# A 31-tap depthwise convolution as three half-length ones on VectorE, inside a two-block kernel

## The chip, the cores and the metric

One NeuronCore of a Trainium2 chip runs the whole program. The metric is the device time of one execution in microseconds; the runs shown are three of the same kernel, and a profiled execution is a fourth. The names of engines are those of the profile: PE is TensorE, DVE is VectorE, ACT is ScalarE, POOL is GpSimd, SP is the queue of SyncE.

## The reference

Two blocks follow each other on x (1024 tokens, width 1024). The first is a mixer, a cross-attention and a squared-ReLU MLP; nothing in it is touched. The second starts with one projection that is cut into nine pieces for four mixers, whose outputs are concatenated, projected and followed by a gated MLP:

```
z_pool, s_b, s_c, s_h, c_a, c_g, zq, zk, zv = split(rms_norm(x) @ w_in)
u      = c_a * sigmoid(c_g)                      # 256 channels
u      = causal_dwconv(u, conf_dw_w) + conf_dw_b # 31 taps, every channel its own
y_conf = silu(layer_norm(u))
y_attn = differential attention: softmax(q1 k1) - lam * softmax(q2 k2), times v   # 4 heads
x      = x + concat(y_pool, y_sconv, y_conf, y_attn) @ w_out
```

The change touches two places: the 31-tap convolution behind `u`, and in the attention the one number per query by which the second softmax is scaled before it is added to the first, `-lam * sum1 / sum2`.

## The kernel before, in words

All activations are kept channels by tokens: a tile of 128 x 1024 f32 holds 128 channels (partitions) and all 1024 tokens. A matrix product splits each f32 operand into a rounded part and a remainder and issues three matmuls of 512 columns per 128 rows of depth; the weight's remainder `wl` is computed by POOL (from `wr` and `wh`), activations' remainders by DVE. DVE reads each product out of PSUM (`gm`).

The program is written as Python generators ("tasks") that a small planner, `drive`, interleaves: it takes the task of the lowest priority number whose awaited tiles are ready by the planner's clock for TensorE, and issues its instructions up to the next `yield`. The clock prices a DVE instruction at 0.065 us plus 1.04 ns a column, a POOL one at 0.05 us plus 2.2 ns a column; it does not let one engine slow another. What it issues is then the order on each engine, up to a short window within which the scheduler may exchange instructions (24 for DVE, 8 for ACT and POOL; PE keeps its order). Each engine takes its instructions strictly in that order.

In `second`, the projection is the task of priority 10, so it fills PE when nothing else is ready. ORDER2 lists its pieces: attention pair 0, convolution 0, sconv 1, convolution 1, sconv 0, attention pair 1, pool 1, pool 0. Heads run as tasks of priority 2, their value part in `attn_value`, and the two convolutions (128 channels each) as tasks of priority 3 in `conf_in`.

`conf_in` (line 2233) gates `ca` with the sigmoid of `cg`, then builds the sum over 31 taps in two accumulators. On DVE, taps 0 to 20: ACT writes tap 0 with the bias into `cy`, and 20 instructions add a shifted and scaled copy of the input, each over about 1010 columns, two of them between two yields (line 2247). On POOL, taps 21 to 30: ACT writes tap 21 into a second accumulator (also named `cy` in the trace), and for each of the other nine ACT makes a scaled copy `ctap` (line 2253) and POOL adds it (line 2254). One DVE addition joins the two accumulators (line 2257). When both convolutions are done, `conf_out` normalises them, and their results go to DRAM and come back for the output projection.

`attn_value` (line 2149) is the tail of one block of 128 queries: a reciprocal of the two row sums (`ars`), the column factor (`ars<-asm,nlam,ars`, one column, line 2157), one DVE instruction that adds the second softmax to the first with that factor (`ap<-ap,ars`, up to 1024 columns, line 2159), then PE transposes the result (`apt`), ACT copies it (`aT`), and PE multiplies by v (`apo`). At the end of a head pair DVE normalises `ao` and PE transposes it (`yaT`).

Of the kernel before, what the change touches and what calls it, by code (L numbers as in the profile page):

```python
# [11 lines left out]
AF = mybir.ActivationFunctionType  # L12
ALU = mybir.AluOpType
# [23 lines left out]
G_CONV, G_ONORM, G_POOL, G_SC, G_CW, G_CB, G_CG, G_CBB, G_QG, G_KG = 56, 104, 105, 107, 113, 175, 177, 179, 181, 182  # L37
# [7 lines left out]


PRI = 200

CONF_POOL = 10

QD = 2

# [150 lines left out]
class Kern:  # L203
# [1945 lines left out]
    def attn_value(self, ao, vT, qt, P, sm, done):  # L2149
        nc = self.nc  # L2150
        n = (qt + 1) * 128

        rs = self.small("ars", 4)
        yield [sm]
        nc.vector.reciprocal(rs[:, 0:2], sm)
        yield [rs]
        nc.vector.scalar_tensor_tensor(rs[:, 2:3], sm[:, 0:1], self.nlam, rs[:, 1:2], ALU.mult, ALU.mult)
        yield [rs]
        nc.vector.scalar_tensor_tensor(P[0], P[1], rs[:, 2:3], P[0], ALU.mult, ALU.add)
        P = P[0]  # L2160
        aT = None
        for c0 in range(0, n, 512):
            c1 = min(n, c0 + 512)
            yield [P, self.free_s()]
            if aT is None:
                aT = self.u("aT")
            pt = self.s("apt")
            for kb in range(0, (c1 - c0) // 128):
                o = c0 + kb * 128
                nc.tensor.transpose(pt[:, kb * 128:kb * 128 + 128], P[:, o:o + 128], self.ident)  # L2170
            nc.scalar.activation(aT[:, c0:c1], pt[:, :c1 - c0], AF.Copy)
        del P
        yield [aT, self.free_s()]
        po = self.s("apo")
        for kb in range(qt + 1):
            nc.tensor.matmul(po[:, 0:64], aT[:, kb * 128:kb * 128 + 128], vT[:, kb * 64:kb * 64 + 64], start=(kb == 0), stop=(kb == qt))
        nc.scalar.activation(ao[:, qt], po[:, 0:64], AF.Copy, scale=rs[:, 0:1])
        done.set(ao)
# [52 lines left out]
        self.y_set(j, y)  # L2231

    def conf_in(self, j, a, g_):
        nc, gv = self.nc, self.gv
        nc.scalar.activation(g_, g_, AF.Sigmoid)
        nc.vector.tensor_tensor(a, a, g_, ALU.mult)
        y, y2 = self.u("cy"), self.u("cy2")
        w = G_CW + 31 * j
        nc.scalar.activation(y, a, AF.Identity, scale=gv[:, w + 30:w + 31], bias=gv[:, G_CB + j:G_CB + j + 1])

        first = 31 - CONF_POOL
        tap = lambda d: gv[:, w + 30 - d:w + 31 - d]
        nc.gpsimd.memset(y2[:, 0:first], 0.0)
        nc.scalar.activation(y2[:, first:], a[:, :1024 - first], AF.Copy, scale=tap(first))
        far = list(range(first + 1, 31))
        for d in range(1, first):
            nc.vector.scalar_tensor_tensor(y[:, d:], a[:, :1024 - d], tap(d), y[:, d:], ALU.mult, ALU.add)
            if d % 2 == 0:
                yield [y]
                if far:  # L2250
                    f = far.pop(0)
                    p = self.u("ctap")
                    nc.scalar.activation(p[:, f:], a[:, :1024 - f], AF.Copy, scale=tap(f))
                    nc.gpsimd.tensor_tensor(y2[:, f:], y2[:, f:], p[:, f:], ALU.add)
        assert not far
        yield [y2]
        nc.vector.tensor_tensor(y, y, y2, ALU.add)
        self.cu[j] = y
        self.ev_cu[j].set(y)

# [160 lines left out]
```

## Time and profile before

| what | value |
|---|---|
| three runs | 2655.64, 2653.11, 2649.26 us, median 2653.11 us |
| the profiled execution | 2642.57 us, of which the span of the trace is 2640.9 us |
| mean granted TensorE clock | 0.981 |
| busy: PE, DVE, ACT, POOL | 2509.0, 1578.5, 871.9, 891.5 us |

Times in the trace are microseconds from the start of the span. Busy PE is the time in which at least one matmul is under way. The second block's projection, attention and convolutions lie at about 1500 to 1900 us. The names `cy` and `pl` occur in other stages too, so a row on them is read with its stretch.

### The profile page before, as it was taken

The page shows a single profiled execution, that of the slowest core. Times are in us where ns is not written, and L with a number is a line of the kernel's source. Part 1 is how long each engine was busy: PE and PEld are TensorE (multiplying, and loading weights), DVE is VectorE, ACT ScalarE, POOL GpSimd, SP SyncE. Part 2 cuts the span into 40 slices and gives each one's busy share as a digit, 9 for nine tenths or more (in the row PEclk, how much of TensorE's full clock was granted, in tenths as well). Part 3 has the DMA queues.
Part 4 walks back from the last instruction along what each step waited for, and adds up shares of the span by engine and source line. Part 5 has one row for each costly group of instructions (what it writes and reads, how often), then busy time and mean ns, then how long its engine had stood idle before and what let it go on. Part 6 is the DMA issues. An engine that isn't in the chain of part 4 may idle for free. (4 is left out here: it accounts for less than half of the span.)

```text
span 2640.9 us, 30371 instructions
## 1 busy us (share of the span) xinstructions
PE 2509.0 (95%) x11880; PEld 2056.6 (78%) x11880; DVE 1578.5 (60%) x2249; ACT 871.9 (33%) x1234; POOL 891.5 (34%) x376
## 2 busy tenths in 40 slices
PE   8999999999999999999999889888969999999999
PEld 6878877888877888778888667667847888887887
DVE  7972767554456666553435767976586666564433
ACT  5422343233343333321213434434453222222210
POOL 1121121211244454322222442521175556653221
PEclk9999999999999999999999999899979999999999
DMA  3322146421232333642211331033221222226212
GB/s 128 88 83 74 64 159 214 170 88 47 70 124 82 118 104 120 231 137 97 97 56 48 118 91 56 32 130 100 78 85 64 88 88 80 80 97 251 91 49 88
DMA packets 99135, 268.26 MB, mean 102 GB/s; under 512 B 19976, under 2 KB 34480, under 8 KB 98992
## 3 DMA queue, kind: packets, MB, share of 16 engines
q1 hardware_dynamic: 78400, 192.40, 21.3%
q10 hardware_dynamic: 20592, 73.93, 8.4%
q8 instruction: 93, 1.52, 0.2%
q14 instruction: 50, 0.41, 0.1%
HBM read 196.55 MB, written 69.74 MB: 101 GB/s over the span
## 5 line engine op out<-in xcount | busy, mean ns | idle before, releaser
L184 POOL TENSOR_TENSOR wl<-wr,wh 128x1024 fp32r<-128x1024 f32 (+1 forms) x137 | 340.9, 2489 | 1299.0 <-ACT wh L184 1235.2
L184 DVE TENSOR_TENSOR x<-gm,x 128x512 f32<-128x512 f32 x304 | 209.0, 688 | 355.9 <-PE gm L184 355.6
L184 ACT ACTIVATE wh<-wr 128x1024 fp32r<-128x1024 f32 (+2 forms) x147 | 153.0, 1042 | 610.0 <-PE gm L184 575.7
L184 PE MATMUL gm<-fhh,wh 128*128 128x512 f32 x864 | 337.7, 391 | 3.4 <-ACT fhh L184 2.5
L184 PE MATMUL gm<-fhl,wh 128*128 128x512 f32 x864 | 337.1, 390 | 1.5 <-DVE fhl L184 1.4
L184 PE MATMUL gm<-fhh,wl 128*128 128x512 f32 x864 | 336.6, 390 | 0.0
L184 PE MATMUL gm<-hh,wh 128*128 128x512 f32 x800 | 325.0, 407 | 11.8 <-ACT hh L184 7.7
L184 PE MATMUL gm<-hl,wh 128*128 128x512 f32 x800 | 319.8, 400 | 0.5 <-DVE hl L184 0.5
L184 PE MATMUL gm<-hh,wl 128*128 128x512 f32 x800 | 319.0, 399 | 0.0
L184 PEld LDWEIGHTS gm<-fhh,wh 128*128 128x128 f32 x864 | 162.2, 188 | 41.5 <-ACT fhh L184 3.3
L184 PEld LDWEIGHTS gm<-fhl,wh 128*128 128x128 f32 x864 | 162.3, 188 | 36.0 <-DVE fhl L184 3.1
L184 PEld LDWEIGHTS gm<-fhh,wl 128*128 128x128 f32 x864 | 162.3, 188 | 33.9
L184 PEld LDWEIGHTS gm<-hh,wh 128*128 128x128 f32 x800 | 153.7, 192 | 44.4 <-ACT hh L184 8.6
L184 PEld LDWEIGHTS gm<-hh,wl 128*128 128x128 f32 x800 | 153.7, 192 | 32.5 <-issue 0.5
L184 PEld LDWEIGHTS gm<-hl,wh 128*128 128x128 f32 x800 | 153.8, 192 | 31.1 <-DVE hl L184 1.9
L184 POOL TENSOR_TENSOR wl<-pr,wh 128x1024 fp32r<-128x1024 f32 x38 | 91.6, 2410 | 118.1 <-ACT wh L184 118.1
L184 POOL TENSOR_TENSOR wl<-sa,wh 128x1024 fp32r<-128x1024 f32 x38 | 92.9, 2446 | 106.5 <-ACT wh L184 106.5
L184 PE MATMUL q<-tl,wh 128*128 128x512 f32 x304 | 120.6, 397 | 6.6 <-POOL tl L184 6.6
L184 PE MATMUL q<-th,wl 128*128 128x512 f32 x304 | 120.7, 397 | 4.6 <-POOL wl L184 4.6
L184 PE MATMUL q<-th,wh 128*128 128x512 f32 x304 | 119.3, 394 | 3.5 <-ACT th L184 2.6
L184 POOL TENSOR_TENSOR pl<-sb,ph 128x1024 fp32r<-128x1024 f32 x38 | 92.8, 2443 | 86.2 <-ACT ph L184 86.1
L184 DVE TENSOR_TENSOR fhl<-fhr,fhh 128x1024 fp32r<-128x1024 f32 x54 | 91.3, 1696 | 29.8 <-ACT fhh L184 29.8
(445 smaller groups left out, 5328.0 us busy)
## 6 DMA issues: line engine op xcount, KB each, us to landing
fhr<-hd SPq DMA_DIRECT2D x54, 512.0 KB, 5.1
wr<-in_w_in_dram ACTq DMA_DIRECT2D x39, 512.0 KB, 3.5
xd<-x SPq DMA_DIRECT2D x32, 512.0 KB, 2.6
x<-xd SPq DMA_DIRECT2D x32, 512.0 KB, 4.6
pr<-in_ffn_w_dram SPq DMA_DIRECT2D x32, 512.0 KB, 3.6
wr<-in_ffn_w_dram ACTq DMA_DIRECT2D x32, 512.0 KB, 3.5
hd<-ft SPq DMA_DIRECT2D x27, 512.0 KB, 5.0
hd<-pc SPq DMA_DIRECT2D x27, 512.0 KB, 5.8
```

The source lines that it names most:

```text
L184: ins = f(*args, **kw)
```

## The change

The convolution is written over even tokens, odd tokens and their sums. With a0 and a1 the even and odd tokens (512 columns each), h0 the 16 even taps and h1 the 15 odd ones, three convolutions over 512 columns are made: p0 = h0 * a0, p1 = h1 * a1, p2 = (h0 + h1) * (a0 + a1). Even outputs are p0 plus p1 delayed by one, odd outputs are p2 - p0 - p1. ACT writes the first tap of each, DVE all others: 15, 14 and 15 instructions, of 497 to 511 columns, three (at the last step two) between two yields. POOL has no part in it any more, and the copies `ctap` are gone. New on DVE are the sums of neighbouring taps (16 columns), the sum a0 + a1, and four instructions that put the result together; the gating multiplication now reads its two inputs at every second column and writes halves, and two of the last four write every second column.

In `attn_value` the column factor is one `tensor_scalar` with two column operands in place of a `scalar_tensor_tensor`.

```diff
-CONF_POOL = 10
...
-        nc.vector.scalar_tensor_tensor(rs[:, 2:3], sm[:, 0:1], self.nlam, rs[:, 1:2], ALU.mult, ALU.mult)
+        nc.vector.tensor_scalar(rs[:, 2:3], sm[:, 0:1], self.nlam, rs[:, 1:2], ALU.mult, ALU.mult)
...
     def conf_in(self, j, a, g_):
         nc, gv = self.nc, self.gv
+        apart = lambda x: x.rearrange("p (n h) -> p h n", h=2)
+        w = G_CW + 31 * j
+        hs = self.small("hs", 16)
+        pairs = gv[:, w + 1:w + 31].rearrange("p (m o) -> p m o", o=2)
+        nc.vector.tensor_tensor(hs[:, 1:16], pairs[:, :, 0], pairs[:, :, 1], ALU.add)
+        nc.vector.tensor_copy(hs[:, 0:1], gv[:, w:w + 1])
         nc.scalar.activation(g_, g_, AF.Sigmoid)
-        nc.vector.tensor_tensor(a, a, g_, ALU.mult)
-        y, y2 = self.u("cy"), self.u("cy2")
-        w = G_CW + 31 * j
-        nc.scalar.activation(y, a, AF.Identity, scale=gv[:, w + 30:w + 31], bias=gv[:, G_CB + j:G_CB + j + 1])
-        first = 31 - CONF_POOL
+        ab = self.u("cab")
+        nc.vector.tensor_tensor(ab.rearrange("p (h n) -> p h n", h=2), apart(a), apart(g_), ALU.mult)
+        yield [ab]
+        sc, y2 = self.u("csc"), self.u("cy2")
+        a0, a1, both = ab[:, :512], ab[:, 512:], sc[:, :512]
+        nc.vector.tensor_tensor(both, a0, a1, ALU.add)
         tap = lambda d: gv[:, w + 30 - d:w + 31 - d]
-        nc.gpsimd.memset(y2[:, 0:first], 0.0)
-        nc.scalar.activation(y2[:, first:], a[:, :1024 - first], AF.Copy, scale=tap(first))
-        far = list(range(first + 1, 31))
-        for d in range(1, first):
-            nc.vector.scalar_tensor_tensor(y[:, d:], a[:, :1024 - d], tap(d), y[:, d:], ALU.mult, ALU.add)
-            if d % 2 == 0:
-                yield [y]
-                if far:
-                    f = far.pop(0)
-                    p = self.u("ctap")
-                    nc.scalar.activation(p[:, f:], a[:, :1024 - f], AF.Copy, scale=tap(f))
-                    nc.gpsimd.tensor_tensor(y2[:, f:], y2[:, f:], p[:, f:], ALU.add)
-        assert not far
-        yield [y2]
-        nc.vector.tensor_tensor(y, y, y2, ALU.add)
+        parts = [(y2[:, :512], a0, lambda k: tap(2 * k), 16), (y2[:, 512:], a1, lambda k: tap(2 * k + 1), 15), (sc[:, 512:], both, lambda k: hs[:, 15 - k:16 - k], 16)]
+        for y, x, t, n in parts:
+            nc.scalar.activation(y, x, AF.Copy, scale=t(0))
+        for k in range(1, 16):
+            for y, x, t, n in parts:
+                if k < n:
+                    nc.vector.scalar_tensor_tensor(y[:, k:], x[:, :512 - k], t(k), y[:, k:], ALU.mult, ALU.add)
+            yield [y2, sc]
+        y = self.u("cy")
+        ya = apart(y)
+        bias = gv[:, G_CB + j:G_CB + j + 1]
+        p0, p1, p2 = (part[0] for part in parts)
+        nc.vector.scalar_tensor_tensor(ya[:, 0, 1:], p0[:, 1:], bias, p1[:, :511], ALU.add, ALU.add)
+        nc.vector.tensor_scalar(ya[:, 0, 0:1], p0[:, 0:1], bias, None, ALU.add)
+        nc.vector.tensor_tensor(p0, p0, p1, ALU.add)
+        nc.vector.scalar_tensor_tensor(ya[:, 1], p2, bias, p0, ALU.add, ALU.subtract)
```

## Rows read from the trace of the kernel before

**Rows 1.** The page, part 1: busy us, share of the span, instructions.

```profile
PE 2509.0 (95%) x11880; PEld 2056.6 (78%) x11880; DVE 1578.5 (60%) x2249; ACT 871.9 (33%) x1234; POOL 891.5 (34%) x376
```

**Rows 2.** Windows: stretch, length, busy PE, PEld, DVE, ACT, POOL, granted clock, DMA, GB/s.

```profile
1541.00:1607.00 66.00, 52.97 (x245) 43.53 (x243) 61.94 (x54) 28.85 (x51) 36.50 (x15) 0.92 0.20 56
1607.00:1651.00 44.00, 41.76 (x253) 35.97 (x252) 29.03 (x51) 22.98 (x52) 4.83 (x3) 1.00 0.14 49
1651.00:1723.00 72.00, 55.08 (x256) 44.95 (x255) 67.34 (x63) 27.07 (x40) 38.20 (x14) 0.91 0.09 29
1820.00:1880.00 60.00, 60.00 (x374) 52.76 (x374) 35.96 (x70) 32.99 (x79) 6.00 (x3) 1.00 0.28 93
```

**Rows 3.** Waits of PE, 1541 to 1723: us in total, times, longest.

```profile
PE apt L184 <- DVE ap L184: 14.8, 5, 4.7
PE apt L184 <- DVE ars L184: 6.1, 2, 4.3
```

**Rows 4.** DVE's groups, 1541 to 1723: out<-in xcount | busy us, mean ns | idle before.

```profile
L184 DVE SCALAR_TENSOR_TENSOR cy<-ca,gv,cy 128x1023 f32<-128x1023 f32 (+19 forms) x40 | 71.5, 1789 | 1.5 <-ACT cy L184 1.2
L184 DVE SCALAR_TENSOR_TENSOR ap<-ap,ars,ap 128x640 f32<-128x640 f32 (+3 forms) x8 | 17.1, 2133 | 0.1
L184 DVE SCALAR_TENSOR_TENSOR ars<-asm,nlam,ars 128x1 f32<-128x1 f32 x16 | 14.1, 888 | 0.2
L184 DVE SCALAR_TENSOR_TENSOR ap<-ap,ars 128x128 f32<-128x128 f32 (+3 forms) x8 | 8.4, 1055 | 0.1
L184 DVE TENSOR_SCALAR ass<-ass 128x8 f32<-128x8 f32 x2 | 2.0, 1006 | 0.0
```

**Rows 5.** Timeline of DVE: start us, us, instruction, count.

```profile
1564.11 2.58 DVE L184 SCALAR_TENSOR_TENSOR cy<-ca,gv,cy 128x1015 f32<-128x1015 f32 x2
...
1566.72 3.32 DVE L184 SCALAR_TENSOR_TENSOR cy<-ca,gv,cy 128x1013 f32<-128x1013 f32 x1
...
1571.11 0.67 DVE L184 TENSOR_TENSOR sh<-gm,sc 128x512 f32<-128x512 f32 x1
1571.70 1.08 DVE L184 SCALAR_TENSOR_TENSOR ars<-asm,nlam,ars 128x1 f32<-128x1 f32 x1
1572.70 1.26 DVE L184 SCALAR_TENSOR_TENSOR cy<-ca,gv,cy 128x1012 f32<-128x1012 f32 x1
1573.89 2.65 DVE L184 SCALAR_TENSOR_TENSOR ap<-ap,ars 128x384 f32<-128x384 f32 x1
...
1714.96 1.23 DVE L184 TENSOR_TENSOR cy<-cy,cy 128x1024 f32<-128x1024 f32 x1 [2.22 <-POOL cy L184]
```

**Rows 6.** Timeline of POOL over the same stretch.

```profile
1566.63 2.35 POOL L184 TENSOR_TENSOR cy<-cy,ctap 128x1000 f32<-128x1000 f32 x1 [2.48 <-ACT ctap L184]
1570.36 2.40 POOL L184 TENSOR_TENSOR wl<-wr,wh 128x1024 fp32r<-128x1024 f32 x1 [1.39 <-ACT wh L184]
1573.82 2.30 POOL L184 TENSOR_TENSOR cy<-cy,ctap 128x999 f32<-128x999 f32 x1 [1.06 <-ACT ctap L184]
```

**Rows 7.** POOL's groups, 1541 to 1723.

```profile
L184 POOL TENSOR_TENSOR cy<-cy,ctap 128x1002 f32<-128x1002 f32 (+8 forms) x18 | 49.4, 2747 | 44.2 <-ACT ctap L184 43.9
L184 POOL TENSOR_TENSOR wl<-wr,wh 128x1024 fp32r<-128x1024 f32 x9 | 22.7, 2517 | 63.4 <-ACT wh L184 63.4
L184 POOL TENSOR_TENSOR sh<-sh,r1b 128x1024 f32<-128x1024 f32 x2 | 6.0, 3019 | 0.0
```

**Rows 8.** DVE's groups by form, 1800 to 1890, where POOL does little.

```profile
L184 DVE SCALAR_TENSOR_TENSOR ars<-asm,nlam,ars 128x1 f32<-128x1 f32 x16 | 3.5, 216 | 0.3
...
L184 DVE SCALAR_TENSOR_TENSOR ap<-ap,ars 128x512 f32<-128x512 f32 x2 | 1.5, 752 | 0.0
```

**Rows 9.** Windows: one wait of PE, and the stretch right behind it.

```profile
1582.50:1586.00 3.50, 0.21 (x2) 0.07 (x1) 3.50 (x3) 0.00 (x0) 2.85 (x1) 1.00 0.99 249
1586.70:1590.10 3.40, 3.40 (x9) 2.64 (x9) 3.40 (x5) 1.17 (x3) 0.00 (x0) 0.50 0.28 70
```

**Rows 10.** The only DVE TENSOR_SCALAR of one full column, by its tile.

```profile
L184 DVE TENSOR_SCALAR nlam<-nlam x1: 145/145/145, 1450.4 to 1450.4; 128x1 f32<-128x1 f32 x1
```

## The prediction, made before the changed kernel ran

> **What bounds the kernel now.** I read the page's first part, then windows over the second block, then PE's waits there, then DVE and POOL side by side in the timeline. PE is busy 95% of the span [rows 1], so time can only come from stretches in which it isn't. The two convolutions are such stretches: PE is busy 52.97 of 66 us and 55.08 of 72 us, 30.0 us idle together, while DVE is busy 94% [rows 2]. Between the two the same attention and projection run with 2.2 us idle in 44, and later with none in 60, DVE being at 66% and 60%: the idle time belongs to a saturated DVE, not to the attention's own chain. PE waits there 20.9 us for two DVE results, `ap` and `ars` [rows 3]; the rest falls on several others. A second loss stands beside it. The granted clock is 0.92 and 0.91 in the two stretches and 1.00 outside [rows 2], which is 66 x 0.08 + 72 x 0.09 = 11.8 us of full-speed work. Right behind a wait of 3.5 us in which PE did 0.21 us of work, a stretch of 3.4 us ran at 0.50, the lower level of 1.2 GHz [rows 9]; the clock fell when PE had stood still.
>
> **Why DVE is saturated.** A tap of 1012 columns takes 1.26 us when it runs freely, and 3.32 us when POOL's addition of a tap, begun 0.09 us before it, is under way: POOL ends at 1568.98, the tap at 1570.04, one free duration later [rows 5, 6]. So does `ap` at 1573.89, behind POOL's 1573.82 [rows 5, 6]. Even the one-column `ars` averages 0.888 us here against 0.216 us where POOL does little [rows 4, 8]. A DVE instruction that reads two SBUF tiles stands until POOL's is over. Reckoned over both stretches, with free durations of 0.752 us at 512 columns and 1.26 at 1012 (1.02 ns a column) [rows 5, 8]: taps 71.5 - 40 x 1.27 = 20.7; the long `ap` (832 columns in the mean, 1.08 us) 17.1 - 8.6 = 8.5; the short ones (320, 0.56 us) 8.4 - 4.4 = 4.0; `ars` 14.1 - 3.5 = 10.6; `ass` about 1.7 [rows 4, 8]. Sum 45.5 us in which DVE stood, of its 129.3 busy. POOL's work there is 49.4 us of taps, 22.7 of `wl` and 6.0 of `sh` [rows 7]; taps are 63%, which gives them 28.8 of the 45.5 us.
>
> **The change part by part.**
>
> *POOL's taps go.* DVE gains 28.8 us over the two convolutions, and ACT loses one copy per tap. DVE's wait of 2.22 us for POOL's last tap, with a head pair's tail queued behind it, goes too [rows 5].
>
> *DVE's taps.* Before, 40 in all; DVE begins the next instruction 0.08 us before the end of one whose result it doesn't need (1571.11 to 1571.70 for 0.67 us), and 0.04 us behind the end of one whose result it does (two taps in 2.58 us) [rows 5]. A tap so occupies 1.19 to 1.31 us; most are followed by another instruction, I take 1.22: 24.5 us per convolution. After, 44 of 504 columns in the mean, 0.742 us each. Three accumulators alternate, so no tap needs the one ahead: 0.66 us, 29.0 per convolution. Should two halves of a tile count as one, it is 0.78, 34.3 per convolution. I take the first, nearest to the 0.59 us of a 512-column instruction in [rows 5]. Difference +4.5, at most +9.8, at least +2.8 per convolution.
>
> *The other additions on DVE, per convolution.* The sum a0 + a1 0.59 us; the two small ones on taps 0.2; at the end two of 0.67, one of 0.59 and one of a column 0.1, against 1.15 for the old join. Together +1.7. The gating multiplication keeps its count of elements. That it and two of the last four step over every second column is in no row; bounds: nothing, or twice their time per element, +2.2. I take nothing, since the row nearest to it, a dense 512-column one, shows no cost but columns. The Trainium skill (SBUF - State Buffer, section "Door 1: The DMA port swizzle") says that reads which meet a 16-byte line at least twice run at full rate; f32 at a step of two does so, and by that page the term is nothing too. No run here shows it yet.
>
> Sum on DVE: 2 x (4.5 + 1.7) = +12.4 against -28.8, net -16 us of 129 (bounds -1 to -20).
>
> *The column factor.* `tensor_scalar` of one column took 145 ns [rows 10], `scalar_tensor_tensor` 216 [rows 8]: 16 x 0.07 = 1.1 us in these stretches if it holds, at most 10.6 if the new form never stands behind POOL. But then `ap`, the next on its chain, stands behind the same POOL instruction instead, and a TENSOR_SCALAR, `ass`, was also held (1.006 us in the mean) [rows 4]. I count nothing.
>
> *ACT and POOL.* ACT's six first taps become half as wide; both engines have room (ACT 28.85 of 66 us, POOL 36.50) [rows 2]. Nothing.
>
> **From DVE to the end.** PE's order is fixed, and it has other work at 100% once its waits are gone (1820 to 1880 in [rows 2]). So what it doesn't wait, the span loses. Of PE's 30.0 us the taps' 63% give 19. The added 12.4 us are in the planner's prices for the most part (0.59 against 0.66 us a tap) and displace attention by little; POOL's blocks are in no price, and that is what made PE late. The clock's 11.8 us goes with the waits in the same share, 7 us. Total 26 us. The new DVE work may bring back some waits: at -1 us net on DVE the gain would be only what smoother order brings, some 5; and with all waits and the whole clock back it would be 42. What is late next: `wl` and `sh`, whose 28.7 us of POOL stay, and then the attention's loads.
>
> The profiled execution took 2642.6 us, the median of the runs is 2653.1, 10.5 higher. By the profile the sum gives 2616.6, on the scale of the runs 2627.
>
> **The rivals.** A measurement of this kernel can tell about 0.2%, 5.3 us, from no change.
>
> *The rest of POOL blocks more.* Nearly every instruction that DVE now has reads two SBUF tiles and is short, so that whenever `wl` or `sh` runs, one stands at the head of the queue. Before, a microsecond of POOL held DVE for 45.5 / 78.1 = 0.58 us. At 1.0, the 28.7 us left hold it for 28.7 instead of 16.7, DVE's relief falls from 16 to 4 us, and the gain in that proportion from 26 to 6.5: 2647. For it: taps make up half of DVE's instructions' time in [rows 4]. Against: DVE also reads PSUM in the projection and the maxima, which did not stand (0.67 at 1571.11 beside a POOL run [rows 5, 6]). The Trainium skill (SBUF - State Buffer, section "Who interferes with whom") has the pair of ports as a lock for a whole instruction, the loser blocked entirely; by that rule the price of a `wl` can't shrink with the width of the tap it meets, and the trace agrees: beside the `wl` of 1570.36 the one-column `ars` took 1.08 us and ended with it [rows 5, 6].
>
> *DVE takes more than it gives back (slower).* Forty-four instructions at their start-to-start cost, alone on DVE, behind which the heads' `ap` queue. Place: the same two stretches. It decides from (16 / 88) + 0.66 = 0.84 us a tap on; 0.78 doesn't reach it, but a step of two charged at each read or a wait on the first ACT tap could. At 1.0 us DVE has 14 us more than before, PE's waits grow by the 30 / 45.5 that a blocked microsecond cost so far, +9 us, and the clock with it: 2665. For: DVE is at 94% already. Against: 0.59 us for 512 columns.
>
> *All comes back.* No wait left, full clock: 2653 - 42 = 2611. For: the stretches without taps. Against: `wl` still holds DVE.
>
> **How the numbers follow.** The forecast (15 to 36 us of gain, own range 2617 to 2638) 0.57; all comes back 0.13; the rest of POOL blocks more, or the planner's new order brings other waits, 0.20, of which two thirds lie within 0.2%; slower 0.10. So faster 0.77, same 0.13, slower 0.10. The range runs from 2610 (nearly all) to 2650 (the weak case): the slower case and the edge of the others stay out.
>
> **What would show it.** In the profile after: no `ctap`, and 88 taps near 0.74 us with starts 0.66 apart; POOL's busy time down by 49 us or more; the sum of `ap` and `ars` near free durations, except beside `wl`; PE's waits for `ap` and `ars` under a third; the granted clock above 0.97 in both stretches. I am wrong if the taps stand 0.8 us apart, if PE's idle time in the convolutions stays near 30 us, or if it reappears between the convolutions and the output projection.

## The result and the profile after

The changed kernel takes 2618.07 us in the median of four runs (2615.66 to 2618.96), the kernel before 2654.29 us in the four beside it (2649.26 to 2655.64). The ratio is 0.9872, 95% interval 0.9855 to 0.9889: 36 us less, where 26 were forecast and 2627 us named, inside the range of 2610 to 2650. The profiled execution after is one of the four, 2618.96 us with a span of 2616.7.

First the windows of the kernel after: the two convolutions, now at 1545 to 1625 and 1625 to 1705, and the stretch behind them (columns as in [rows 2]).

```profile
1545.00:1625.00 80.00, 75.66 (x408) 63.39 (x406) 71.99 (x109) 32.57 (x72) 15.36 (x7) 1.00 0.22 66
1625.00:1705.00 80.00, 73.50 (x391) 60.72 (x389) 77.56 (x119) 30.52 (x59) 16.48 (x7) 1.00 0.15 51
1705.00:1723.00 18.00, 12.06 (x39) 8.49 (x40) 16.21 (x35) 5.86 (x7) 4.67 (x2) 0.72 0.02 10
```

PE's idle time in the convolutions is 4.34 + 6.50 = 10.8 us, against 30.0 in [rows 2], and the granted clock is 1.00 in both instead of 0.92 and 0.91. DVE is no less busy than before, 90% and 97% against 94%: what fell is not its busy share but PE's waits for what comes out of it. These windows don't hold the same work as those of [rows 2]: the matmuls that stood in the 44 us between the two convolutions now run inside them. The third window shows what is left: PE is idle 5.94 us behind the convolutions, and there the clock falls to 0.72. PE's waits from 1545 to 1723 say the same, against 20.9 us for `ap` and `ars` in [rows 3]; `ars` is gone from the list.

```profile
PE apt L182 <- DVE ap L182: 7.1, 3, 3.0
PE gm L182 <- DVE zqk L182: 2.9, 2, 2.3
PE cm L182 <- DVE zv L182: 2.4, 1, 2.4
```

The groups of DVE from 1535 to 1725, which answer to [rows 4]. The taps of p0 and p1 are named `cy`, those of p2 `csc`; the row `cab<-ca,cg` is the gating, which reads at every second column, and `cy<-csc,gv,cy` the odd outputs, written at every second column.

```profile
L182 DVE SCALAR_TENSOR_TENSOR cy<-cab,gv,cy 128x511 f32<-128x511 f32 (+14 forms) x58 | 47.3, 841 | 0.0
L182 DVE SCALAR_TENSOR_TENSOR csc<-csc,hs 128x511 f32<-128x511 f32 (+14 forms) x30 | 26.1, 869 | 0.0
...
L182 DVE SCALAR_TENSOR_TENSOR ap<-ap,ars,ap 128x640 f32<-128x640 f32 (+3 forms) x8 | 8.6, 1077 | 0.0
...
L182 DVE SCALAR_TENSOR_TENSOR ap<-ap,ars 128x128 f32<-128x128 f32 (+3 forms) x8 | 6.2, 772 | 0.1
...
L182 DVE TENSOR_SCALAR ars<-asm,nlam,ars 128x1 f32<-128x1 f32 x16 | 4.3, 266 | 0.1
...
L182 DVE TENSOR_TENSOR cab<-ca,cg 128x1024 f32<-128x1024 f32 x2 | 2.4, 1216 | 2.6 <-ACT cg L182 2.6
...
L182 DVE SCALAR_TENSOR_TENSOR cy<-csc,gv,cy 128x512 f32<-128x512 f32 x2 | 1.5, 748 | 0.0
```

The eight long `ap` have come from 17.1 us down to 8.6, their free time; `ars` from 14.1 to 4.3. The timelines of DVE and of POOL over one stretch show the taps in step and what still holds them: taps begin 0.66 us apart (1560.40, 1561.06, and two in 1.32), until POOL's `wl` and `sh` stand in the way of two of them (1566.28 and 1568.55).

```profile
1560.40 0.74 DVE L182 SCALAR_TENSOR_TENSOR csc<-csc,hs 128x511 f32<-128x511 f32 x1
1561.06 1.41 DVE L182 SCALAR_TENSOR_TENSOR cy<-cab,gv,cy 128x510 f32<-128x510 f32 x2
1562.38 0.74 DVE L182 SCALAR_TENSOR_TENSOR csc<-csc,hs 128x510 f32<-128x510 f32 x1
...
1566.28 2.35 DVE L182 SCALAR_TENSOR_TENSOR cy<-cab,gv,cy 128x508 f32<-128x508 f32 x1
1568.55 2.88 DVE L182 SCALAR_TENSOR_TENSOR csc<-csc,hs 128x508 f32<-128x508 f32 x1
```

```profile
1565.70 2.39 POOL L182 TENSOR_TENSOR wl<-wr,wh 128x1024 fp32r<-128x1024 f32 x1 [9.22 <-ACT wh L182]
1568.04 2.85 POOL L182 TENSOR_TENSOR sh<-sh,r1b 128x1024 f32<-128x1024 f32 x1
```

The gain lies in one stretch. From the first transpose of the attention's norms (`zb`) to the first matmul of the output projection (`gm<-yh,wh`) the kernel before takes 295.3 us and the kernel after 264.7, which is 30.6 less (the two profiles differ by 24.2 us in all; experiment 4 takes up the rest). These are the windows of that stretch, first before, then after. PE's records of matmuls are as many in both, 1223, so here like is compared with like: its idle time falls from 41.5 to 20.1 us, and its busy time, which a lower clock lengthens, from 253.8 to 244.6.

```profile
1498.20:1793.50 295.30, 253.76 (x1223) 206.92 (x1224) 219.77 (x275) 118.35 (x188) 113.07 (x45) 0.94 0.28 88
```

```profile
1501.50:1766.20 264.70, 244.56 (x1223) 200.51 (x1224) 208.27 (x336) 97.53 (x170) 61.96 (x25) 0.96 0.31 98
```

### The profile page after: what moved, and what is told of

The parts are those of the page before. It is cut to its first block, busy times and chain, and to the rows that moved or that the text cites. A ratio compares the mean times of both kernels' runs of the same rounds, so it can differ in the third digit from the quotient of the medians.

```text
span 2616.7 us, 30367 instructions
## 1 busy us (share of the span) xinstructions
PE 2500.9 (96%) x11880; PEld 2053.4 (78%) x11880; DVE 1564.9 (60%) x2309; ACT 853.3 (33%) x1218; POOL 840.0 (32%) x356
```

## The experiments

Theory: POOL's additions of taps, which read SBUF, made DVE's instructions on two SBUF tiles stand, `ap` and `ars` among them, for which PE waited. Rivals: fewer copies on ACT; a finer order through half-length taps; less work on DVE; the column factor. Times are medians; "before" is the kernel before, run beside each experiment. "Stretch" is the one just named.

**1. POOL writes, but reads nothing.**

```diff
-                    nc.gpsimd.tensor_tensor(y2[:, f:], y2[:, f:], p[:, f:], ALU.add)
+                    nc.gpsimd.memset(self.u("cz")[:, f:], 0.0)
```

> The kernel before, with one thing changed: where POOL added a tap (it read two SBUF tiles), it now fills a scratch tile with zeros, so it only writes. ACT's copies, DVE's 20 full-width taps per convolution and the planner's prices stay. Taps 22 to 30 are left out of the result. Theory (POOL's reads hold DVE): DVE's taps come down from 1.79 us to about 1.35 in the mean, since only wl and sh still hold them, DVE gets some 29 us back and the time falls by 25 to 40 us against before, 2614 to 2629. Rival (the gain comes from fewer ACT copies, from halving the taps or from a smoother order): no more than 5 us, 2648 or above, taps still near 1.8 us.

2619.41 us, ratio 0.9868 (0.9844 to 0.9892), as much as the whole change, with DVE's full-width taps and ACT's copies in place. The groups of POOL and of DVE, 1541 to 1723:

```profile
L184 POOL MEMSET cz<- 128x1002 f32 (+8 forms) x18 | 16.2, 930 | 0.0
...
L184 DVE SCALAR_TENSOR_TENSOR cy<-ca,gv,cy 128x1023 f32<-128x1023 f32 (+19 forms) x40 | 53.6, 1340 | 0.5
```

The taps' mean is 1.34 us instead of 1.79. So none of the rivals is needed for the size of the gain. But POOL is also less busy here, 16.2 us of fills against 49.4 of additions, so that reading and being busy aren't told apart yet.

**2. All 30 taps on DVE at full width.**

```diff
-        first = 31 - CONF_POOL
...
-        for d in range(1, first):
+        for d in range(1, 31):
...
-                if far:
...
-        yield [y2]
-        nc.vector.tensor_tensor(y, y, y2, ALU.add)
```

> The kernel before with all 30 further taps on DVE at full width, two between two yields, no POOL and no copies: the same result as before, without the half-length form. Theory: POOL's 29 us of holding are gone, but 20 more taps of 1.2 us, 24 us, come to DVE; the net is about 5 us less DVE, and as the planner prices the added taps but not the holding, the time falls by 5 to 20 us against before, 2634 to 2649. Then the half-length form is worth the rest, 16 to 31 us. Rival (taking POOL out is all that counts, DVE's own sum isn't): as the changed kernel, 2618 within 5.

2631.20 us, ratio 0.9908 (0.9884 to 0.9932): faster than before by 22 us, 3 us better than the theory's 5 to 20 against the 2653.75 us beside it, and 13 us slower than with half-length taps, where 16 to 31 were expected. Adding 20 taps to DVE still pays, since they only take its time, while POOL's additions hold its queue. DVE's taps, 1545 to 1720:

```profile
L184 DVE SCALAR_TENSOR_TENSOR cy<-ca,gv,cy 128x1023 f32<-128x1023 f32 (+29 forms) x60 | 86.2, 1437 | 0.6
```

**3. The old companions back, to no use, in the changed kernel.**

```diff
+            if k < 10:
+                p = self.u("ctap")
+                nc.scalar.activation(p[:, 21 + k:], ab[:, :1003 - k], AF.Copy, scale=tap(21 + k))
+                nc.gpsimd.tensor_tensor(z[:, 21 + k:], z[:, 21 + k:], p[:, 21 + k:], ALU.add)
```

> The changed kernel with the old companions put back, to no use: for each convolution ACT makes nine scaled copies of about 1000 columns, and POOL adds them into a scratch tile that nobody reads. Theory: DVE, which now has 12 us more of its own work than before, is held by POOL again for about 29 us, PE's waits for ap come back, and the time rises by 25 to 45 us, to 2643 to 2663, near or above before. Rival (halved taps and their finer order made the gain): within 8 us of the changed kernel, below 2626.

2653.06 us, ratio to before 0.9998 (0.9985 to 1.0012). The whole gain is gone, though the halved taps and their finer order are all there. `ars` is never held in this run, and `ap` only little; what the additions hold are above all the taps, which take 94.3 us in place of 73.4, and PE waits for `ap` all the same. POOL's additions, DVE's taps and PE's waits, 1545 to 1740:

```profile
L182 POOL TENSOR_TENSOR cz<-cz,ctap 128x1002 f32<-128x1002 f32 (+8 forms) x18 | 46.5, 2582 | 56.2 <-ACT ctap L182 47.8 <-DMA stk<-qkd 8.0
```

```profile
L182 DVE SCALAR_TENSOR_TENSOR cy<-cab,gv,cy 128x511 f32<-128x511 f32 (+14 forms) x58 | 53.8, 948 | 0.0
L182 DVE SCALAR_TENSOR_TENSOR csc<-csc,hs 128x511 f32<-128x511 f32 (+14 forms) x30 | 40.5, 1350 | 0.0
...
L182 DVE SCALAR_TENSOR_TENSOR ap<-ap,ars,ap 128x640 f32<-128x640 f32 (+3 forms) x8 | 12.2, 1520 | 0.0
L182 DVE SCALAR_TENSOR_TENSOR ap<-ap,ars 128x128 f32<-128x128 f32 (+3 forms) x8 | 6.3, 782 | 0.1
...
L182 DVE TENSOR_SCALAR ars<-asm,nlam,ars 128x1 f32<-128x1 f32 x16 | 4.2, 262 | 0.0
```

```profile
PE apt L182 <- DVE ap L182: 20.8, 5, 8.5
PE gm L182 <- DVE ca L182: 6.0, 1, 6.0
PE gm L182 <- DVE zqk L182: 4.0, 1, 4.0
```

**4. The kernel before, profiled again.** Nothing is edited.

> The kernel before, unchanged, for a second profile: the one shown took 2642.6 us, the runs 2649 to 2656. If the ten microseconds lie in the convolutions, then how POOL's and DVE's instructions meet varies from run to run: PE's idle time there is 35 to 40 us instead of 30. If they lie elsewhere (loads, the second MLP), the idle time in the convolutions is 30 within 2, and the gain of the change on the scale of the profiles is the 24 us that the two profiles show.

2652.92 us, the usual time of that kernel. Its windows over the stretches of [rows 2], and over the stretch from `zb` to the output projection:

```profile
1541.00:1607.00 66.00, 52.31 (x242) 43.27 (x241) 58.28 (x53) 29.77 (x50) 37.30 (x15) 0.90 0.20 56
1607.00:1651.00 44.00, 42.11 (x251) 36.44 (x250) 28.15 (x50) 22.81 (x54) 5.27 (x3) 0.96 0.11 37
1651.00:1723.00 72.00, 57.52 (x273) 46.83 (x271) 68.46 (x52) 28.07 (x41) 39.20 (x16) 0.93 0.12 37
```

```profile
1502.90:1800.30 297.40, 254.68 (x1224) 208.84 (x1224) 219.15 (x275) 118.30 (x188) 114.94 (x45) 0.92 0.28 88
```

PE is idle 28.2 us in the convolutions (13.7 and 14.5), within 2 of the 30 of the first profile, so the 10 us don't lie there. They are spread: the stretch begins at 1502.9 us instead of 1498.2, takes 297.4 instead of 295.3, and what follows it takes 3.5 more. But the expectation was wrong to take the two profiles' 24 us for the gain then: the profile before was a quick one throughout. Against this one, at the kernel's usual time, the change shortens the stretch by 297.4 - 264.7 = 32.7 us, of 34.5 us in all.

**5. Writes for as long as the additions took.** To experiment 3, with fills in place of additions, three for each, of which the planner prices one (`_e` passes it by).

```diff
-                nc.gpsimd.tensor_tensor(z[:, 21 + k:], z[:, 21 + k:], p[:, 21 + k:], ALU.add)
+                z2 = self.u("cz2")
+                nc.gpsimd.memset(z2[:, 21 + k:], 0.0)
+                for _ in range(2):
+                    nc.gpsimd._e.memset(z2[:, 21 + k:], 0.0)
```

> As the run before with POOL's useless additions in the changed kernel, ACT's 18 copies kept, but each POOL addition replaced by three fills of a scratch tile with zeros (0.93 us each in an earlier run, so about 50 us of POOL in all, as the additions took), which only write. Theory (only POOL's reads hold DVE): 2618 to 2625, taps' mean below 0.9 us, as in the changed kernel. Rival (ACT's extra copies, or POOL being busy at all and late for wl, made the 35 us): 2640 to 2655.

2618.38 us, ratio to before 0.9872 (0.9859 to 0.9884): the changed kernel's time to the half microsecond. POOL spends 33.1 + 16.8 us on fills, as long as on the additions before, ACT makes all its copies, and DVE's taps take 73.2 us, as if none of this were there (73.4 in the changed kernel). POOL's and DVE's groups, 1545 to 1705 (the fills stand in two rows, since they were issued from two lines):

```profile
L2265 POOL MEMSET cz<- 128x1002 f32 (+8 forms) x36 | 33.1, 933 | 1.1
...
L182 POOL MEMSET cz<- 128x1002 f32 (+8 forms) x18 | 16.8, 933 | 3.2 <-PE apt L182 3.1
```

```profile
L182 DVE SCALAR_TENSOR_TENSOR cy<-cab,gv,cy 128x511 f32<-128x511 f32 (+14 forms) x58 | 48.9, 862 | 0.0
L182 DVE SCALAR_TENSOR_TENSOR csc<-csc,hs 128x511 f32<-128x511 f32 (+14 forms) x30 | 24.3, 809 | 0.0
```

Together with experiment 3 this settles it: it is POOL's reading of SBUF, not its being busy and not ACT's copies, that costs 35 us. The planner's order is no rival either: in the traces of experiments 3 and 5 all but 11 of PE's 11880 instructions, all but 3 of DVE's 2309 and all of ACT's stand in the same sequence. The stretch in experiment 3, then in 5, shows what the additions cost DVE:

```profile
1504.90:1800.90 296.00, 256.26 (x1218) 211.34 (x1218) 233.94 (x336) 119.11 (x192) 106.37 (x43) 0.90 0.28 88
```

```profile
1503.30:1767.20 263.90, 243.02 (x1216) 199.67 (x1217) 200.80 (x336) 119.10 (x192) 108.82 (x79) 0.97 0.31 99
```

The Trainium skill (SBUF - State Buffer, section "Who interferes with whom") says that a DVE instruction with two SBUF inputs contends with a GpSimd instruction that reads SBUF, and not with one that only writes it. The traces of the two runs agree with both halves: the `csc` taps take 1.35 us in the mean beside the additions and 0.81 us beside the fills.

**6. and 7. The column factor, alone in the kernel before, and taken back in the changed one.**

```diff
-        nc.vector.scalar_tensor_tensor(rs[:, 2:3], sm[:, 0:1], self.nlam, rs[:, 1:2], ALU.mult, ALU.mult)
+        nc.vector.tensor_scalar(rs[:, 2:3], sm[:, 0:1], self.nlam, rs[:, 1:2], ALU.mult, ALU.mult)
```

> The kernel before with only the column factor as tensor_scalar. In the changed kernel that form took 256 to 277 ns in all 32 cases, never longer, while the old one took 204 to 2334. Theory (ap stands behind the same POOL instruction instead): DVE's time in ars falls by 10 us and most of it comes back in ap; within 4 us of before, 2650 to 2658. Rival (the released factor lets DVE do other work, and takes a part of the gain): 6 to 10 us faster, 2644 to 2648.

2649.79 us, ratio 0.9991 (0.9982 to 1.0001): 2 us, which the interval doesn't set apart from none, and within the theory's 4 us. `ars` and the long `ap` in the kernel with the factor alone, the first by its tile, the others in the stretch 1545 to 1730:

```profile
L184 DVE TENSOR_SCALAR ars<-asm,nlam,ars x32: 255/272/276, 1565.5 to 1885.8; 128x1 f32<-128x1 f32 x32
```

```profile
L184 DVE SCALAR_TENSOR_TENSOR cy<-ca,gv,cy 128x1023 f32<-128x1023 f32 (+19 forms) x40 | 74.3, 1857 | 1.5 <-ACT cy L184 1.2
...
L184 DVE SCALAR_TENSOR_TENSOR ap<-ap,ars,ap 128x640 f32<-128x640 f32 (+3 forms) x8 | 19.2, 2395 | 0.1
...
L184 DVE TENSOR_SCALAR ars<-asm,nlam,ars 128x1 f32<-128x1 f32 x16 | 4.2, 268 | 0.1
```

`ars` gives back 9.9 us, and of it the taps take 2.8 and the long `ap` 2.1: half of it goes to what comes next on DVE, which the same POOL instructions now hold (one profile of each kernel).

> The changed kernel with the column factor back as scalar_tensor_tensor. Theory: the old form is 0.055 us shorter when free and held by wl or sh in one or two of 32 cases, so nothing to be seen: within 3 us of the changed kernel, 2615 to 2621. Rival (the factor carries a part of the gain): 2622 to 2628.

2619.52 us (2615.10 to 2625.16), 1.5 us above the changed kernel. The old factor is held more often than the one or two times that were expected, and still the time doesn't follow. Its row, 1541 to 1705, against 4.3 us in the changed kernel:

```profile
L182 DVE SCALAR_TENSOR_TENSOR ars<-asm,nlam,ars 128x1 f32<-128x1 f32 x16 | 10.4, 650 | 0.1
```

The factor has no part in the gain that these runs can tell.

**8. The weights' remainders on DVE too.** To the changed kernel, for the eleven pieces whose weights are prepared during the convolutions.

```diff
+        self.wvec |= set(range(101, 112))
```

> The changed kernel with the weight remainders wl of eleven projection pieces (those loaded while the convolutions run) computed on DVE in 1.2 us each in place of POOL's 2.4. POOL still multiplies sh and adds csum. Theory: DVE takes on 13 us of work, which the planner prices, and is rid of some 18 us of holding, which it doesn't; PE's 7 us of waits for ap shrink: 2606 to 2617, faster by up to 12. Rival (DVE at 97% in the second convolution is simply full, and a wl that waits in its queue makes PE wait for the weight): 2620 to 2632.

2608.35 us, ratio to before 0.9837 (0.9824 to 0.9850): 10 us below the changed kernel, as the theory had it. DVE computes each `wl` in half of POOL's time, and its `csc` taps run free, at 0.739 us. PE is busy 156.75 of 159 us in the convolutions, where the changed kernel has 148.84 (window and DVE's groups, 1541 to 1700 and 1541 to 1705):

```profile
1541.00:1700.00 159.00, 156.75 (x836) 132.32 (x836) 142.71 (x234) 66.95 (x133) 6.75 (x2) 1.00 0.20 60
```

```profile
L182 DVE SCALAR_TENSOR_TENSOR csc<-csc,hs 128x511 f32<-128x511 f32 (+14 forms) x30 | 22.2, 739 | 0.0
L182 DVE TENSOR_TENSOR wl<-wr,wh 128x1024 fp32r<-128x1024 f32 x10 | 12.2, 1220 | 0.3 <-ACT wh L182 0.2
```

The longest waits of PE that are left, 1498 to 1760, lie outside the convolutions:

```profile
PE pp L182 <- DVE pld L182: 6.6, 1, 6.6
PE zb L182 <- ACT zbr L182: 6.5, 1, 6.5
```

**9. Nothing on POOL during the convolutions.** To experiment 8, with two more kinds of POOL's work on DVE.

```diff
-        nc.gpsimd.tensor_tensor(sh, sh, self.rb2, ALU.mult)
+        nc.vector.tensor_tensor(sh, sh, self.rb2, ALU.mult)
...
-        nc.gpsimd.tensor_tensor(cs, cu[0], cu[1], ALU.add)
+        nc.vector.tensor_tensor(cs, cu[0], cu[1], ALU.add)
```

> As the kernel with wl of eleven pieces on DVE, with sh's multiplications and the first csum on DVE too, so that POOL reads nothing while the convolutions run. Theory: PE was idle only 2.3 us of 159 there, so what is left to win by freeing DVE is 2 us at most: 2604 to 2612, no difference that can be told. Rival (DVE, at 96% in the second convolution, tips over): 2613 to 2622.

2622.45 us, 14 us worse than experiment 8 and half a microsecond above what even the rival allowed. But its place was not where the rival put it: DVE does not tip over, being busy 140.39 us there against 142.71, and PE is idle only 2 us more (154.60 of 159 us, below). The profiled execution, 2617.76 us, is the fastest of its four and 9 us slower than that of experiment 8: the stretch takes 6.2 us more (260.0 against 253.8), what follows it 6.1 us more, and what is ahead of it 3.1 us less. PE's longest wait from 1541 to 1770, the one for `pld`, is shorter than in experiment 8 (4.6 us against 6.6), so it doesn't explain the loss. Where the 14 us come from is open.

```profile
1541.00:1700.00 159.00, 154.60 (x819) 130.82 (x818) 140.39 (x231) 66.98 (x133) 0.00 (x0) 0.99 0.20 60
```

```profile
PE pp L182 <- DVE pld L182: 4.6, 1, 4.6
```

**10. `wl` on DVE from the projection's first piece to the output projection.** To experiment 8, with 26 pieces.

```diff
-        self.wvec |= set(range(101, 112))
+        self.wvec |= set(range(96, 122))
```

> As the kernel with wl of eleven pieces on DVE, but for 26 pieces, from the first of the second block's projection to those of its output projection. Theory: outside the convolutions DVE isn't the engine that PE waits for, so nothing is gained; DVE's added work meets the split of the mixers' outputs: 2606 to 2616. Rival (POOL holds DVE on PE's path there too): 2598 to 2605.

2595.64 us (2594.61 to 2598.41), ratio to before 0.9784 (0.9772 to 0.9797): the rival's side, a little better than it said, and the best of all, 22 us below the changed kernel. The stretch takes 242.5 us, with POOL busy 21.65 us in it and 32 matmuls fewer (1191 against 1223), which have moved ahead of it or behind it. Its window, and PE's wait for `pld`:

```profile
1498.50:1741.00 242.50, 233.22 (x1191) 193.52 (x1189) 197.73 (x345) 94.56 (x166) 21.65 (x8) 0.98 0.34 104
```

```profile
PE pp L182 <- DVE pld L182: 1.5, 1, 1.5
```

So taking the remainders off POOL pays outside the convolutions too. In what way isn't shown. The long waits of experiment 8 for `pld` and `zbr` have shrunk to 1.5 us and none. But POOL also copies a part of the tiles `pl` from which `pld` is made, so a `wl` ahead of such a copy in POOL's own queue would delay `pld` without holding DVE. How much of the last 13 us is holding, how much POOL's queue and how much the planner's new order was not separated.

## Why the prediction was right, step by step

**POOL's reads hold DVE: shown.** Experiments 1, 3 and 5 turn the holding off, on and off again, and the time follows by 34, 35 and 35 us.

**The relief on DVE was over-sized, by a little.** Forecast were 28.8 us less holding out of 45.5. By the same reckoning the groups after, 1535 to 1725, hold 73.4 - 88 x 0.735 = 8.7 us of taps and 1.9 of `ap`; and 15 or so of short instructions (`ry`, `rq`, `ao`, `scy`, `yl` and others, each held once or twice). That is about 25 us left, beside 38.5 us of POOL's reads: each of these costs 0.66 us, against 0.58 before, and at that rate the 28.7 us of the forecast would hold 19 us, not 17. The rival of a POOL that blocks more said 28.7. The runs can't tell 0.66 from 0.58: experiment 5 has the same reads of POOL in its stretch, and there DVE is busy 200.80 us, in the changed kernel 208.27. Experiment 3 prices the additions themselves: with the same 336 instructions, DVE is busy 233.94 - 208.27 = 25.7 us longer than in the changed kernel for 46.5 us of additions, 0.55 us for each of them (33.1 us and 0.71 against experiment 5).

**Both terms of the sum were too small.** Over the stretch PE's idle time fell by 21.4 us (by 22.6 against the second profile), where 19 were forecast, and its busy time, for the same matmuls, by 9.2 us (10.1), which is put down to the clock and for which 7 were forecast. Together this is the 30.6 us (32.7) by which the stretch shortened. In the windows of the convolutions alone the idle time fell by 30.0 - 10.8 = 19.2 us, just the forecast; that is luck, since those windows hold different work. So the mechanism was right and both sizes were low. The forecast took its shares from the two convolutions alone, while the stretch had 41.5 us of idle time in all; which of it came back can't be told place by place, since the matmuls stand in another order after. How much of PE's waiting follows from a microsecond of DVE's holding is open too. The prediction gives a reason, that POOL's blocks were in no price of the planner's, but no run has a planner that prices them.

**It is not `ap` and `ars` being held themselves.** They stood 23.1 us before and 1.9 after, which suggests that PE waits only for what is held on its own chain. Experiments 3 and 7 speak against it. In experiment 3 `ars` is free and the long `ap` is held 3.6 us more than in the changed kernel, while the taps take 20.9 us more; PE waits 20.8 us for `ap`, and the whole gain is gone. In experiment 7 `ars` stands 10.4 - 3.5 = 6.9 us, and no loss can be told. What fits both, though no run shows it by itself, is the prediction's own picture: `ap` waits in DVE's queue behind held taps.

**The clock.** In the two convolutions the granted clock is 1.00 after; the drops that had followed PE's waits there did not occur; behind the convolutions it still falls (0.72 in 18 us). Shorter waits alone do not explain it: before, the clock fell to 0.50 behind a wait of 2.04 us, at 1695.9, while after, the longest wait for `ap`, 3.0 us, was followed by none. The runs leave open what made the difference.

**DVE's own work was priced well.** Taps take 0.72 to 0.73 us when free (0.742 forecast) and start 0.66 us apart. Steps of two cost nothing: the gating multiplication takes 1.216 us as it did with dense reads (1.217, its row before, 1541 to 1723, below), the odd outputs 0.748 us for 512 columns (0.752 in [rows 8]). That took the ground from the rival in which DVE takes more than it gives.

```profile
L184 DVE TENSOR_TENSOR ca<-ca,cg 128x1024 f32<-128x1024 f32 x2 | 2.4, 1217 | 2.5 <-ACT cg L184 2.5
```

**The column factor was mispriced, with no effect.** It takes 0.27 us, not 0.145, so it is slower than the 0.216 before when both run freely; the row of 0.145 us [rows 10] has a constant where this one has two columns. But it was never held, in 32 of 32 cases, and the prediction's reason for counting nothing, that what comes next stands instead, is what experiment 6 shows for about half of it.

**The scale.** The profile before ran 10 us faster than that kernel's usual time. Taking the sum off the runs' median, 2627 us, and not off the profile, 2616.6, was the right choice, though the latter lies nearer to what was measured: it does so only because the gain was 10 us larger than forecast. Experiment 4 shows the profile's 10 us to be spread over the whole program.

## What to carry to other kernels

Before giving POOL a share of elementwise work, look at what DVE does at that time: where POOL reads SBUF and DVE's instructions read two SBUF tiles, the work ran in front of DVE's and not beside it, and a one-column instruction waited as long as a wide one (0.888 us in the mean against 0.216 [rows 4, 8]). More work on DVE can be faster than less work beside a reading POOL: 20 full-width taps added on DVE, in place of POOL's 18 additions, made this kernel 22 us faster. And read a stretch's idle PE time and granted clock together: here the waits brought back 21 us and the clock behind them 9.

## What the runs showed of the hardware

- A POOL addition of 1000 columns held a DVE instruction with two SBUF inputs until it ended (a tap of 3.32 us in place of 1.26 [rows 5, 6]); POOL fills of the same width, 0.93 us each and 50 us in all, did not (taps of 0.81 and 0.86 us in the mean, experiment 5).
- A `tensor_scalar` of one column with two column operands took 246 to 284 ns in every profile that has it and was never held, though 12 of them ran wholly within a read of POOL's, while a `scalar_tensor_tensor` on the same data took up to 2.38 us (experiment 7), and a `tensor_scalar` of 8 columns with constants was held too (`ass`, 1.006 us in the mean in [rows 4], 0.170 us where POOL does little).
- DVE read or wrote f32 at every second column at the rate of dense ones: 1.216 us against 1.217 for 1024 columns read, 0.748 against 0.752 for 512 written.
